# The weights of the first norm: one row and two matmuls in place of a load of 128 equal rows

## The chip, the cores and the metric

The kernel runs on 1 core of one Trainium2 chip. The metric is the device time of one execution in microseconds (us). The kernel before took 2623.56 us (median of 3 runs, 2621.81 to 2627.48 us).

## What is computed

One layer of an encoder trunk on a sequence of 2048 frames with 1024 features, all in float32: token mixing (one projection of the normed input, whose columns go to sliding-window attention with sinks and to a gated linear recurrence, then one output projection), cross-attention into 256 memory tokens, and a SwiGLU feed-forward part. Each of the three stands between two RMS norms with their own weights. The change touches the first norm of all:

```python
def rms_norm(x, g):
    xf = x.astype(jnp.float32)
    y = xf * lax.rsqrt(jnp.mean(xf * xf, axis=-1, keepdims=True) + RMS_EPS)
    return (y * g.astype(jnp.float32)).astype(x.dtype)

    u = rms_norm(h, g_mix_pre[l])
    z = u @ w_in[l]
    ...
```

`g_mix_pre` is one row of 1024 float32 numbers, drawn around 1.

## The kernel before

The work is written against a tile framework: the program lists instructions with the tiles that they read and write, and a planner, which simulates the engines' times, orders the instructions of each engine, picks the buffers and sets all semaphores. So the order on an engine may differ from the order of the text. Each engine then runs its own list strictly in order. All loads and stores of this stage are issued by one queue, that of SyncE (SP), and also in order.

Every large product is done in three float32r matmuls: each operand is split into a high part (a copy rounded to float32r) and a low part (what is left), and high x high, high x low and low x high are added in PSUM (`products`, L1017 to L1019). Most products go block by block through a seven-product scheme, the first two blocks of the input projection through a plain one (`eight`).

`in_first` (L413) does the first half of the input projection, 1024 frames in two groups `s` of four tiles of 128 frames. A frame lies in a partition, so a tile is 128 x 1024 and the norm's weights have to stand in all 128 partitions. The steps of the first 40 us are:

- `x_loads` (L418) loads tiles of x, 512 KB each, into `stage[s]`, a tile of 128 x 4 x 1024 with the tag "T" (three buffers, which the split operands of later blocks use after it). Right behind the first tile of x, it calls `gain` (L88), which loads the weights into the tile `g_mix` from a source with a zero step over the partitions: 128 equal rows of 4 KB, 512 KB in all. All these loads pass through `load`, L75.
- `x0_j`, called `junk`, is the second tile of tag "T". Its only use is to take the squares that nobody reads.
- `normed` (L406) norms one tile in place: ScalarE squares it into `junk` and sums (L409), GpSimd makes the reciprocal root in two small operations (`rstd`, L102 and L104), and VectorE multiplies x by the root and by `g_mix` (L411). The 16 tiles of the first and the second half (L411 in both cases) all read `g_mix`.
- `flipped` (L431) transposes the normed tile on TensorE (L440) into two PSUM banks. `first` (L452) splits them into the high and low parts (L457 on ScalarE, L458 on VectorE); `copied` and `later` keep a float32 copy for later sums (L446) and split that (L888 on GpSimd, L889 on VectorE).
- The weights of the projection (`in_w_in`) come in blocks of 512 rows x 256 columns as `sraw` and are split into `S` by `streamed` and `split2` (L886 on ScalarE or L888 on GpSimd, then L889 on VectorE).

PSUM in this stage has six banks with the tag "m" and two with the tag "s"; `bank("s")` and `bank("h")` both take the latter two in turn.

Of the kernel before, what the change touches and what calls it, by code (L numbers as in the profile page):

```python
# [11 lines left out]
F32 = mybir.dt.float32  # L12
F32R = mybir.dt.float32r
I32 = mybir.dt.int32
AF = mybir.ActivationFunctionType
# [3 lines left out]
P = 128  # L19
T = 2048  # L20
D = 1024
# [15 lines left out]
def f32(ap):  # L37
    return ap.bitcast(F32)
# [10 lines left out]
class Layer:  # L49
# [363 lines left out]
    def in_first(self):  # L413

        nc, I = self.nc, self.I
        stage = []

        def x_loads(s, tiles):  # L418
            if tiles[0] == 0:
                stage.append(self.tb.tile([P, 4, D], F32, tag="T", name=f"x0_{s}", bufs=3))  # L420
            for i in tiles:
                self.load(stage[s][:, i, :], I["x"][(4 * s + i) * P:(4 * s + i + 1) * P, :])
                if s + i == 0:
                    self.g_mix = self.gain(I["g_mix_pre"])

        x_loads(0, (0, 1))
        junk = self.tb.tile([P, 4, D], F32, tag="T", name="x0_j", bufs=3)
        T, raw = {}, {}
        key = {(0, 0): 1, (1, 0): 2, (0, 1): 8, (1, 1): 3}

        def flipped(s, i, kinds):  # L431

            x = stage[s][:, i, :]
            self.normed(x, junk[:, i, :])
            banks = []
            for q in range(2):
                ps = self.bank(kinds[q])
                for j in range(4):
                    k = 4 * q + j
                    nc.tensor.transpose(ps[:, j * P:(j + 1) * P], x[:, k * P:(k + 1) * P], self.ident)  # L440
                banks.append(ps.rearrange("p (j t) -> p j t", j=4))
            return banks

        def copied(s, i, banks):
            for q in range(2):
                nc.scalar.activation(raw[q, s][:, :, i * P:(i + 1) * P], banks[q], AF.Copy)  # L446

        def parts(s, i, q):
            o = slice(i * P, (i + 1) * P)
            return T[key[q, s]][:, 0, :, o], T[key[q, s]][:, 1, :, o]  # L450

        def first(i, kinds):  # L452

            banks = flipped(0, i, kinds)
            for q in range(2):
                hi, lo = parts(0, i, q)
                nc.scalar.activation(hi, banks[q], AF.Copy)  # L457
                nc.vector.tensor_tensor(lo, banks[q], f32(hi), ALU.subtract)  # L458
            return banks

        def later(i):
            banks = flipped(1, i, "sh")
            copied(1, i, banks)
            for q in range(2):
                self.split2(raw[q, 1][:, :, i * P:(i + 1) * P], *parts(1, i, q), "P")

        for s in range(2):
            for q in range(2):
                self._n += 1
                raw[q, s] = self.pair_tile().rearrange("p a d -> p (a d)").rearrange("p (k t) -> p k t", k=4)  # L470
        for q in range(2):
            for s in range(2):
                T[key[q, s]] = self.big.tile([P, 2, 4, 512], F32R, tag="big", name=f"u0_{q}{s}")
        second = {}

        def fetch():
            for s in range(2):
                for q in range(2):
                    r = self.pair_tile().rearrange("p a d -> p (a d)").rearrange("p (k t) -> p k t", k=4)
                    self.load(r, self.un_d[4 * q:4 * q + 4, :, s * 512:(s + 1) * 512].rearrange("k p t -> p k t"))  # L480
                    second[q, s] = r
                    yield

        beside = [(), (0,), (1, 2), (3,), (4,), (5,), (6,), (7,), (), (), ()]
        get = fetch()
        blocks = [("q" if i == 0 else "p" if i < 2 else "s",)
                  + self.in_block(*p, beside[i], get if i > 9 else (), None if i else lambda: x_loads(0, (2, 3)))
                  for i, p in enumerate(self.ORDER)]
        phases = self.phases([(lambda i, j, a, n: raw[i, j][:, a:a + n, :], 4, blocks, None, {})], T)
        next(phases)  # L490
        x_loads(1, range(4))
        b0 = first(0, "sh")
        b1 = first(1, "gt")
        next(phases)
        b2 = first(2, "gt")
        copied(0, 0, b0)
        b3 = first(3, "sh")
        copied(0, 1, b1)
        copied(0, 2, b2)
        copied(0, 3, b3)  # L500
        next(phases)
        for i in range(4):
            later(i)
        self.mix_consts()
        for _ in phases:
            pass
        for _ in get:
            pass
        u = []
        for s in range(2):  # L510
            u.append([])
            for q in range(2):
                self._n += 1
                t = self.big.tile([P, 2, 4, 512], F32R, tag="big", name=f"u1_{q}{s}")
                r = second[q, s]
                for k in (0, 2):
                    self.split2(r[:, k:k + 2], t[:, 0, k:k + 2], t[:, 1, k:k + 2], "A")
                u[s] += [(t[:, 0, k, :], t[:, 1, k, :]) for k in range(4)]
        return u
# [1090 lines left out]
```

## Time and profile before

| | us | share of the span |
|---|---|---|
| median of 3 runs | 2623.56 | |
| the profiled execution | 2629.38 | |
| its span | 2627.7 | |
| TensorE matmuls busy | 2560.7 | 97% |
| VectorE busy | 1732.1 | 66% |
| ScalarE busy | 1262.0 | 48% |
| GpSimd busy | 431.3 | 16% |

In the rows of the profile, PE is TensorE, PEld its loads of stationary operands, DVE VectorE, ACT ScalarE, POOL GpSimd, and SPq the queue of SyncE that issues loads and stores. A row of the timeline has the start in us from the start of the span, the duration in us (from the first to the last of the instructions that were merged into it), the engine, the line, the operation, what it writes and reads, and how many instructions it stands for; in brackets is the time for which the engine had been idle before it, and what ended that. A row of DMA issues has the destination and source, the issuing queue, the count, the size, and the median time in us from issue to landing. A row of the windows has the stretch, its length, the busy time of each engine in it with the count of instructions, the granted clock of TensorE (1.00 is full), the busy share of the DMA engines and the rate.

The first 40 us read so: four loads are issued at once; x tile 0 lands and is squared; the weights land; VectorE norms; TensorE transposes; and the products of the first block begin at 16.82 us.

### The profile page before, as it was taken

The numbers are of one execution on the slowest core, as the hardware profiler recorded it, in microseconds if no ns is written. First come the engines' busy times: TensorE is split into PE (matmuls) and PEld (weight loads), VectorE is DVE, ScalarE is ACT, GpSimd is POOL, SyncE is SP. The second block draws the span as 40 slices with busy tenths as digits, with TensorE's granted clock in tenths as the row PEclk, the third lists the DMA queues.
The fourth block names the chain that finished last, engine by engine and source line by source line (L and its number), as shares of the span: only waits on it lengthen the run. The fifth ranks groups of instructions, "written<-read, shape, count | busy, mean of one in ns | idle before, by whom it ended". The sixth has DMA issues, their size and how long they took to land.

```text
span 2627.7 us, 34806 instructions
## 1 busy us (share of the span) xinstructions
PE 2560.7 (97%) x12329; PEld 2142.2 (82%) x12329; DVE 1732.1 (66%) x2725; ACT 1262.0 (48%) x2628; POOL 431.3 (16%) x627
## 2 busy tenths in 40 slices
PE   7999999999999999999989999999999999999998
PEld 6877888878988887888878888888888888888886
DVE  7675478877545778777676655566666556564656
ACT  5463366655545566565563333344333334453543
POOL 4231344331311332213310000000000000000022
PEclk9999999999999999999999999999999999999999
DMA  5445655675877886666884632353566434576888
GB/s 184 127 149 174 187 158 159 197 232 158 239 256 261 306 279 235 216 233 176 242 276 131 196 101 82 102 191 123 168 203 197 155 121 172 183 215 177 268 209 216
DMA packets 354158, 502.87 MB, mean 191 GB/s; under 512 B 20672, under 2 KB 237760, under 8 KB 353984
## 3 DMA queue, kind: packets, MB, share of 16 engines
q1 hardware_dynamic: 345632, 470.24, 55.0%
q0 software_dynamic: 8352, 30.41, 6.6%
q8 instruction: 97, 1.59, 0.3%
q14 instruction: 77, 0.63, 0.1%
HBM read 338.05 MB, written 162.53 MB: 191 GB/s over the span
## 4 chain that ended last, share of the span: by engine, by line
PE 81%; DMA 8%; DVE 4%; ACT 3%; issue 2%; POOL 1%; SPq 1%; DVEq 0%; POOLq 0%; ACTq 0%
PE psm L1017 23%; PE psm L1018 23%; PE psm L1019 23%; PE psg L158 2%; PE psg L157 2%; PE psg L156 2%; PE pss L1252 1%; DMA qd<-z_d 1%; DMA z<-in_w_out_dram 1%; DMA u_d<-row 1%; DMA qq<-z_d 1%; SPq L75 1%; DVE wlo L889 0%; DMA h_d<-row 0%; DMA row<-y_d 0%
## 5 line engine op out<-in xcount | busy, mean ns | idle before, releaser
L1017 PE MATMUL psm<-T,S 128*128 128x512 f32 x2699 | 1046.6, 392 | 18.7 <-ACT part L1032 9.4
L1018 PE MATMUL psm<-T,S 128*128 128x512 f32 x2699 | 1052.6, 391 | 0.7 <-DVE T L889 0.6
L1019 PE MATMUL psm<-T,S 128*128 128x512 f32 x2699 | 1042.7, 391 | 2.0 <-DVE S L889 2.0
L1017 PEld LDWEIGHTS psm<-T,S 128*128 128x128 f32 x2699 | 508.2, 188 | 129.7 <-ACT part L1032 10.6
L1019 PEld LDWEIGHTS psm<-T,S 128*128 128x128 f32 x2699 | 508.2, 188 | 108.3 <-DVE S L889 2.9
L1018 PEld LDWEIGHTS psm<-T,S 128*128 128x128 f32 x2699 | 508.3, 188 | 106.1 <-DVE T L889 2.1
L889 DVE TENSOR_TENSOR S<-sraw,S 128x512 fp32r<-128x512 f32 (+1 forms) x320 | 218.4, 689 | 215.9 <-ACT S L886 198.6
L886 ACT ACTIVATE S<-sum 128x512 fp32r<-128x512 f32 (+1 forms) x310 | 186.5, 620 | 345.0 <-PE psm L1019 257.9
L889 DVE TENSOR_TENSOR S<-sum,S 128x512 fp32r<-128x512 f32 (+1 forms) x368 | 246.8, 681 | 58.0 <-ACT S L886 34.6
L1032 ACT ACTIVATE part<-psm 128x512 f32<-128x512 f32 x270 | 159.9, 596 | 244.8 <-PE psm L1019 229.3
L886 ACT ACTIVATE S<-sraw 128x512 fp32r<-128x512 f32 (+1 forms) x273 | 168.0, 616 | 120.9 <-PE psm L1019 104.7
L1365 POOL DMA_DIRECT2D row<-y_d x28 | 25.8, 921 | 1124.4 <-DVE row L1541 1032.7
L889 DVE TENSOR_TENSOR T<-row,T 128x1024 fp32r<-128x1024 f32 (+1 forms) x122 | 143.7, 1191 | 66.5 <-ACT T L886 66.0
L156 PE MATMUL psg<-u,whi 128*128 128x512 f32 x352 | 141.5, 402 | 1.6 <-POOL whi L888 1.6
L158 PE MATMUL psg<-u,wlo 128*128 128x512 f32 x352 | 140.2, 398 | 0.9 <-DVE wlo L889 0.9
L157 PE MATMUL psg<-u,whi 128*128 128x512 f32 x352 | 140.3, 398 | 0.0
L886 ACT ACTIVATE T<-row 128x1024 fp32r<-128x1024 f32 x122 | 122.1, 1027 | 23.9 <-DVE row L915 7.8
L1336 ACT ACTIVATE junk<-row 128x512 f32<-128x512 f32 x160 | 99.9, 625 | 67.6 <-DVE row L1358 26.8
L888 POOL TENSOR_SCALAR S<-sum 128x512 fp32r<-128x512 f32 x58 | 48.3, 832 | 288.4 <-PE psm L1019 228.9
L1492 DVE TENSOR_TENSOR row<-psm,part 128x512 f32<-128x512 f32 x63 | 41.7, 688 | 59.5 <-PE psm L1019 59.4
L1501 DVE TENSOR_TENSOR part<-psm,part 128x512 f32<-128x512 f32 x60 | 39.8, 688 | 61.1 <-PE psm L1019 60.9
L156 PEld LDWEIGHTS psg<-u,whi 128*128 128x128 f32 x352 | 66.7, 189 | 14.7 <-POOL whi L888 2.1
(335 smaller groups left out, 3634.0 us busy)
## 6 DMA issues: line engine op xcount, KB each, us to landing
sraw<-in_w_gate_dram SPq DMA_DIRECT2D x44, 512.0 KB, 3.9
sraw<-in_w_up_dram SPq DMA_DIRECT2D x44, 512.0 KB, 4.0
hid_d<-row SPq DMA_DIRECT2D x44, 512.0 KB, 2.6
h_d<-row SPq DMA_DIRECT2D x32, 512.0 KB, 5.8
y_d<-row SPq DMA_DIRECT2D x32, 512.0 KB, 3.2
sraw<-hid_d SPq DMA_DIRECT2D x32, 512.0 KB, 5.1
row<-h_d POOLq DMA_DIRECT2D x30, 512.0 KB, 6.8
row<-u_d SPq DMA_DIRECT2D x30, 512.0 KB, 6.1
```

Source lines behind the costliest of these rows:

```text
L156: nc.tensor.matmul(ps, ah, bh, start=(i == 0), stop=False)
L157: nc.tensor.matmul(ps, ah, bl, start=False, stop=False)
L158: nc.tensor.matmul(ps, al, bh, start=False, stop=(i == n - 1))
L886: self.nc.scalar.activation(hi, raw, AF.Copy)
L888: self.nc.gpsimd.tensor_scalar(hi, raw, 1.0, 1.0, ALU.mult, ALU.mult)
L889: self.nc.vector.tensor_tensor(lo, raw, f32(hi), ALU.subtract)
L1017: nc.tensor.matmul(ps, s[:, 0, k, :], t[:, 0, k, :], start=st, stop=False, **kw)
L1018: nc.tensor.matmul(ps, s[:, 0, k, :], t[:, 1, k, :], start=False, stop=False, **kw)
L1019: nc.tensor.matmul(ps, s[:, 1, k, :], t[:, 0, k, :], start=False, stop=sp, **kw)
L1032: nc.scalar.activation(t, ps, AF.Copy)
L1336: self.nc.scalar.activation(junk, a, AF.Square, scale=float(D) ** -0.5, accum_out=to)
L1492: nc.vector.tensor_tensor(d, a, c, ALU.add)
```

## The change

The weights are loaded as one row of 4 KB into partition 0 of `junk`, ahead of the tiles of x. A row of 128 ones is written beside it. For each half of 512 columns, TensorE multiplies the ones (as a stationary operand of 1 x 128) with the half row (1 x 512) into a bank of the tag "s", which gives 128 equal rows, and ScalarE copies the bank to `g_mix`. Both operands are float32, so the weights pass unsplit. `junk` is asked for before `stage[0]`, so the two exchange places in the order of the "T" tiles.

```diff
             for i in tiles:
                 self.load(stage[s][:, i, :], I["x"][(4 * s + i) * P:(4 * s + i + 1) * P, :])
-                if s + i == 0:
-                    self.g_mix = self.gain(I["g_mix_pre"])
-
+
+        junk = self.tb.tile([P, 4, D], F32, tag="T", name="x0_j", bufs=3)
+
+        row, ones = junk[0:1, 2, :], junk[0:1, 3, 0:P]
+        self.load(row, I["g_mix_pre"][0:1, :])
         x_loads(0, (0, 1))
-        junk = self.tb.tile([P, 4, D], F32, tag="T", name="x0_j", bufs=3)
+        nc.vector.memset(ones, 1.0)
+        self.g_mix = self.gain_tile()
+        for q in range(2):
+            ps = self.bank("sh"[q])
+            sl = slice(q * 512, (q + 1) * 512)
+            nc.tensor.matmul(ps, ones, row[:, sl], start=True, stop=True)
+            nc.scalar.activation(self.g_mix[:, sl], ps, AF.Copy)
         T, raw = {}, {}
```

## The prediction

> **What bounds the kernel now.** I read the page's busy times first, then the busy time by stretches of the span.
>
> ```profile
> span 2627.7 us, 34806 instructions
> PE 2560.7 (97%) x12329; PEld 2142.2 (82%) x12329; DVE 1732.1 (66%) x2725; ACT 1262.0 (48%) x2628; POOL 431.3 (16%) x627
> ```
> ```profile
> core 0: us, PE busy (x) PEld busy (x) DVE busy (x) ACT busy (x) POOL busy (x), PEclk, DMA share, GB/s
> 11.00:27.90 16.90, 13.37 (x78) 12.48 (x79) 16.76 (x23) 13.95 (x28) 11.06 (x16) 1.00 0.96 285
> ...
> 40.00:110.00 70.00, 70.00 (x317) 58.08 (x318) 50.24 (x59) 30.27 (x49) 13.70 (x20) 1.00 0.49 156
> 110.00:700.00 590.00, 569.58 (x3050) 483.75 (x3049) 435.28 (x896) 321.04 (x808) 181.75 (x257) 0.99 0.60 178
> 700.00:1000.00 300.00, 288.77 (x1611) 249.39 (x1610) 188.81 (x232) 165.66 (x364) 70.40 (x102) 0.99 0.82 273
> ```
>
> The kernel as a whole is bound by matmuls: TensorE is busy for 97% of the span, and for 70.00 of 70 us between 40 and 110 us. But the change lies in the first 10 us, and there the limit is another one: from 11 to 27.9 us VectorE is busy for 16.76 of 16.90 us. So the question is when VectorE's unbroken run of work begins, and whether the matmuls behind it move with it. The timeline answers the first part. It is shown by engine: ScalarE, GpSimd, VectorE, TensorE.
>
> ```profile
> 4.08 1.06 ACT L409 ACTIVATE x_j<-x 128x1024 f32<-128x1024 f32 x1 [2.00 <-DMA x<-in_x_dram]
> 5.04 0.19 ACT L409 ACTIVATION_READ_ACCUMULATOR x_j<-x 128x1 f32 x1
> 7.85 1.06 ACT L409 ACTIVATE x_j<-x 128x1024 f32<-128x1024 f32 x1 [2.63 <-DMA x<-in_x_dram]
> ...
> 5.59 0.56 POOL L104 TENSOR_TENSOR n_r<-n_v,mhalf 128x1 f32<-128x1 f32 x1
> 8.91 0.62 POOL L888 TENSOR_SCALAR S<-sraw 128x512 fp32r<-128x512 f32 x1 [2.76 <-DMA sraw<-in_w_in_dram]
> 10.39 0.56 POOL L104 TENSOR_TENSOR n_r<-n_v,mhalf 128x1 f32<-128x1 f32 x1
> ...
> 6.62 1.28 DVE L411 SCALAR_TENSOR_TENSOR x<-x,n_r,g 128x1024 f32<-128x1024 f32 x1 [5.00 <-DMA g<-in_g_mix_pre_dram]
> 9.56 0.69 DVE L889 TENSOR_TENSOR S<-sraw,S 128x512 fp32r<-128x512 f32 x1 [1.66 <-POOL S L888]
> 10.98 1.28 DVE L411 SCALAR_TENSOR_TENSOR x<-x,n_r,g 128x1024 f32<-128x1024 f32 x1 [0.73 <-POOL n_r L104]
> 26.59 1.28 DVE L458 TENSOR_TENSOR u<-pss,u 128x512 fp32r<-128x512 f32 x2
> ...
> 27.33 0.39 PE L1018 MATMUL psm<-u,S 128*128 128x256 f32 x1 [1.22 <-DVE u L458]
> 39.87 0.98 PE L1017 MATMUL psm<-u,S 128*128 128x512 f32 x3 [0.93 <-POOL u L888]
> ```
>
> The load of the weights ends a wait of 5.00 us on VectorE at 6.62, and that is what the change takes away. It isn't the gate, though: GpSimd had the root of tile 0 ready at 5.59 + 0.56 = 6.15, so only 0.47 us of the wait is the weights' own, and VectorE then idles again. Its unbroken run begins with the norm of tile 1 at 10.98. Behind that stand the root of tile 1 (10.39) and, in GpSimd's order, the split of the first weight block (8.91), which waited for its DMA; the squares of tile 1 (7.85) waited for a DMA too. At the far end of the run, the split at 26.59 releases TensorE at 27.33, and TensorE's last wait of this stretch ends at 39.87. With no idle time in the 70 us after that, a shift of VectorE's run should arrive at the end one for one.
>
> **What is removed: 512 KB in the queue.** The issues on SP's queue, and then their times to landing (x tile 0, the weights, x tile 1, the first weight block):
>
> ```profile
> 0.80 0.39 SPq L75 DMA_DIRECT2D x<-in_x_dram  x1
> 1.24 0.42 SPq L75 DMA_DIRECT2D g<-in_g_mix_pre_dram  x1
> 1.71 0.42 SPq L75 DMA_DIRECT2D x<-in_x_dram  x1
> 2.18 1.12 SPq L75 DMA_DIRECT2D sraw<-in_w_in_dram  x2
> ```
> ```profile
> x<-in_x_dram SPq DMA_DIRECT2D x1, 512.0 KB, 3.3
> ...
> g<-in_g_mix_pre_dram SPq DMA_DIRECT2D x1, 512.0 KB, 5.3
> ...
> x<-in_x_dram SPq DMA_DIRECT2D x1, 512.0 KB, 6.1
> ...
> sraw<-in_w_in_dram SPq DMA_DIRECT2D x1, 256.0 KB, 6.7
> ...
> lb<-in_hgrn_lb_dram SPq DMA_DIRECT2D x1, 4.0 KB, 8.9
> ...
> on_raw<-in_hgrn_onorm_dram SPq DMA_DIRECT2D x1, 0.5 KB, 5.1
> ```
>
> Issue plus landing gives 0.80 + 3.3 = 4.10 for x tile 0, 1.24 + 5.3 = 6.54 for the weights, 1.71 + 6.1 = 7.81 for x tile 1 and 2.18 + 6.7 = 8.88 for the weight block: the 512 KB of weights took 6.54 - 4.10 = 2.44 us of the queue, the equal 512 KB of x behind them 7.81 - 6.54 = 1.27 us. Without them, all that comes later lands between 1.27 us (if they cost as x does) and 2.44 us earlier: x tile 1 at 5.4 to 6.5, the weight block at 6.4 to 7.6. One issue takes the place of another, so x tile 1 is issued when it was. Only x tile 0 goes behind the row, by one issue (1.24 - 0.80 = 0.44 us), and lands at 4.1 to 4.54.
>
> **What is added: row, matmuls, copies.** No row of the trace shows a 4 KB load on an empty queue. The bounds are the shortest load or store of all that touch a tile named g, 2.1 us, and x tile 0 with its 512 KB, 3.3 us; the small loads above, 5.1 and 8.9 us, stood in a full queue and serve for a rival. I take 2.5 us, nearer to the shortest since the row has the queue to itself, and the row lands at 0.80 + 2.5 = 3.3 (2.9 to 4.1).
>
> ```profile
> DMA to landing us min/median/max: 2.1/4.7/10.3
> ```
> ```profile
> 7.96 1.97 PE L440 MATMUL pss<-ident,x 128*128 128x128 f32 x8 [7.96 <-DVE x L411]
> 22.09 1.03 PE L440 MATMUL pss<-ident,x 128*128 128x128 f32 x8
> ...
> 361.65 1.46 PE L785 MATMUL psh<-qq,k 128*128 128x192 f32 x8
> ...
> 19.38 0.60 ACT L446 ACTIVATE pair<-psm 128x512 f32<-128x512 f32 x1
> ...
> 1.00 0.48 DVE L368 MEMSET reset<- 128x512 f32 x1
> ```
>
> The ones cost VectorE less than the 0.48 us of a memset of four times the width, in its idle time before 6.62. For a plain float32 matmul of 512 columns, the nearest row is L785: eight records in 1.46 us, two to a matmul, so 0.365 us for 192 columns and 0.97 us for 512. That was with TensorE warm. The same eight transposes took 1.97 us at 7.96 and 1.03 us at 22.09, so an array that has just begun works 1.91 times slower, and the two matmuls cost 1.86 us each. A lower bound is 0.39 us, the matmul of 256 columns at 27.33. With 1.8 us each: the first ends at 5.1, the second at 6.9. A copy of 128x512 out of PSUM takes 0.60 us, so `g_mix` is complete at 7.5; with all lower bounds at 2.9 + 2 x 0.39 + 0.6 = 4.3, with all upper ones at 4.1 + 2 x 1.86 + 0.6 = 8.4. Before, it was 6.54.
>
> [...]
>
> **The sum.** ScalarE runs its list in order, so it matters where the planner puts the two copies. That it moves work is seen in the memset at 1.00, whose text stands behind all of this stage. If the squares of tile 0 aren't held by both copies, they run at about 4.5 to 5.7 or behind the first copy to 6.9, and tile 0 is normed when `g_mix` is there, at some 7.6 to 8.9. Squares with the sum behind them take 5.04 + 0.19 - 4.08 = 1.15 us. Those of tile 1 need x at 5.4 to 6.5 and follow the second copy, from 7.5 to 8.65. From their end (7.85 + 1.15 = 9.0) to the norm it takes 10.98 - 9.0 = 1.98 us now, because the split of the weight block is in GpSimd's way; without it the root is there 6.15 - 5.23 = 0.92 us after the squares, and that block now lands by 7.6 and is split before. So tile 1 is normed at about 9.5 in place of 10.98: **1.5 us earlier**. This lies inside the 1.27 to 2.44 us by which the DMAs behind move up, so the later tiles follow. ScalarE's 1.2 us of copies and TensorE's 3.7 us lie in time in which both wait for x (4.08, 7.96); without that cover each would cost its own length. The exchange of the "T" buffers costs nothing:
>
> ```profile
> 21.86 1.09 ACT L409 ACTIVATE x_j<-x 128x1024 f32<-128x1024 f32 x1
> ...
> 42.00 3.50 DVE L915 TENSOR_TENSOR pair<-pair,pair 128x1024 f32<-128x1024 f32 x3
> ```
>
> `junk` is last written at 21.86, and the work for the first new "T" tile begins at 42.00; if it had to wait, the next late thing would be the split at L886. The term is then 0 - 1.5 = -1.5 us, with bounds 0 and -2.44. The profiled execution, 2629.38 us (1.7 us more than its span), would become 2627.9. It is 5.8 us above the median and above all three runs, so I put the same shift on the median: 2623.56 - 1.5 = **2622.1 us**, 2621 to 2623.6 by the bounds.
>
> **The rivals.** *The copies stand ahead of all squares* (they do in the text). Then tile 0 is squared at 7.5 to 8.65, its root is there at 9.6, it is normed from 9.6 to 10.9, and tile 1 follows at 10.9: as before, 2623.5 us. The transfer is saved and the time is spent on ScalarE. For it speaks the text's order; against it, that x tile 0 lands at 4.5, when ScalarE has nothing else to do.
>
> *The row lands late.* The same order on ScalarE, but the row takes as long as the small loads in the trace: with 5.1 us `g_mix` is complete at 10.1 and all moves by 2.6 us, with 8.9 us at 13.9 and by 6.4 us: 2626.2 to 2630.0 us, slower. It decides from the moment when `g_mix` is later than 7.5 and ScalarE is held by it. Against it: both small loads were issued into a queue that was moving 285 GB/s, and the row comes first.
>
> *The planner orders later work differently.* The change shifts its simulated times at the very start, and its choices depend on them. Nothing can be gained from 40 to 110 us, but TensorE idles for 590 - 569.58 = 20.4 us and 300 - 288.77 = 11.2 us in the two stretches from 110 to 1000 us, where attention and recurrence run beside the projections. A different order there that removes a quarter of these 31.6 us gives about 2615.6, one that adds a quarter 2631.5. For it speaks that the order is made by simulation; against it, that TensorE's 70 full microseconds let the other engines fall back to the same state relative to it.
>
> **How the numbers follow.** A measurement of this kernel can tell about 0.2%, 5.2 us, from no change: its three runs spread over 5.7 us. Forecast 0.38 and the copies ahead 0.18 both end within it. The late row has 0.07, 0.03 of it beyond 5.2 us. The other order has 0.37: 0.16 faster, 0.15 slower, 0.06 within. So faster 0.16, same 0.38 + 0.18 + 0.04 + 0.06 = 0.66, slower 0.15 + 0.03 = 0.18. The range must hold 0.8, so it takes in both ends of the other order at a quarter of the idle time and a little beyond, 2613 to 2633 us; the forecast's own range is 2621 to 2623.6.
>
> **What the changed profile would show.** The row lands near 3.3 us; two matmuls of about 1.8 us and two copies of 0.6 us before 7.6 us; x tile 1 lands at 5.4 to 6.5; VectorE's unbroken run begins near 9.5 and the release of TensorE that was at 27.33 comes near 25.8; from 40 us on all rows have the same order, some 1.5 us earlier. The prediction is wrong if tile 1 is normed after 10.98, if the 1.5 us are there at 40 us and gone at 110 us, or if TensorE's idle time from 110 to 1000 us differs from 31.6 us by more than 5 us.

## The result and the profile after

The changed kernel took 2634.32 us in the median of 18 runs (2626.75 to 2640.36), the kernel before 2628.40 us beside it (18 runs, 2621.81 to 2632.98). The ratio is 1.0023, with a 95% interval of 1.0014 to 1.0031: **6.0 us slower** (3.7 to 8.1, the interval times 2628.4). The profiled execution took 2635.37 us. Its head of the page, and its windows (columns as before):

```profile
span 2633.7 us, 34818 instructions
PE 2561.5 (97%) x12333; PEld 2140.2 (81%) x12333; DVE 1732.8 (66%) x2726; ACT 1262.7 (48%) x2630; POOL 435.2 (17%) x627
```
```profile
11.00:27.90 16.90, 14.94 (x92) 14.16 (x91) 15.79 (x23) 13.59 (x28) 9.45 (x16) 1.00 0.86 257
40.00:110.00 70.00, 69.31 (x307) 57.46 (x308) 49.08 (x58) 29.72 (x48) 14.12 (x19) 0.96 0.44 143
110.00:700.00 590.00, 567.82 (x3048) 481.83 (x3048) 436.98 (x897) 323.08 (x811) 185.78 (x258) 0.99 0.60 178
700.00:1000.00 300.00, 286.70 (x1625) 247.84 (x1623) 188.48 (x233) 164.94 (x362) 71.01 (x102) 1.00 0.82 273
```

The busy times are those of before; no engine has more to do. What stands out is the second window: TensorE is granted 0.96 of its clock from 40 to 110 us, where it had 1.00. The stage that the change edits, in the timeline of the changed kernel (lines of the code behind the edit are 8 higher than before): TensorE, ScalarE, GpSimd, VectorE.

```profile
2.32 3.75 PE L434 MATMUL pss<-x_j 1*128 1x512 f32 x4 [2.32 <-DMA x_j<-in_g_mix_pre_dram]
...
5.18 1.06 ACT L409 ACTIVATE x_j<-x 128x1024 f32<-128x1024 f32 x1 [3.11 <-DMA x<-in_x_dram]
6.24 0.58 ACT L435 ACTIVATE g<-pss 128x512 f32<-128x512 f32 x1
6.71 1.04 ACT L409 ACTIVATE x_j<-x 128x1024 f32<-128x1024 f32 x1
7.75 0.58 ACT L435 ACTIVATE g<-pss 128x512 f32<-128x512 f32 x1
...
7.41 0.62 POOL L896 TENSOR_SCALAR S<-sraw 128x512 fp32r<-128x512 f32 x1 [0.16 <-DMA sraw<-in_w_in_dram]
8.89 1.48 POOL L104 TENSOR_TENSOR n_r<-n_v,mhalf 128x1 f32<-128x1 f32 x1
...
8.67 1.28 DVE L411 SCALAR_TENSOR_TENSOR x<-x,n_r,g 128x1024 f32<-128x1024 f32 x1
10.40 1.28 DVE L411 SCALAR_TENSOR_TENSOR x<-x,n_r,g 128x1024 f32<-128x1024 f32 x1 [0.45 <-POOL n_r L104]
26.54 0.69 DVE L466 TENSOR_TENSOR u<-pss,u 128x512 fp32r<-128x512 f32 x1
```

The row does its part: the weights are complete at 7.75 + 0.58 = 8.33, and tile 1 is normed at 10.40 in place of 10.98. But at 26.54 VectorE begins the last of these splits, which it began at 26.59 before: little is left of the gain, and the lists of the two kernels no longer agree. Two losses lie behind it. The first is at 30 to 48 us. TensorE and the granted clock, before and then after:

```profile
37.78 1.15 PE L1252 MATMUL pss<-ident,pair 128*128 128x128 f32 x8 [0.19 <-ACT pair L446]
```
```profile
34.00:41.00 7.00, 5.42 (x37) 4.06 (x36) 6.07 (x6) 4.36 (x8) 6.08 (x7) 1.00 0.07 19
41.00:44.00 3.00, 3.00 (x15) 2.46 (x14) 2.97 (x4) 0.68 (x1) 0.00 (x0) 1.00 0.47 133
```
```profile
35.03 1.15 PE L448 MATMUL pss<-ident,x 128*128 128x128 f32 x8 [0.20 <-ACT pair L454]
37.04 0.66 PE L448 MATMUL pss<-ident,x 128*128 128x128 f32 x4 [0.86 <-ACT pair L454]
40.69 1.65 PE L1025 MATMUL psm<-u,S 128*128 128x512 f32 x3 [2.99 <-POOL u L896]
46.37 1.04 PE L1260 MATMUL pss<-ident,pair 128*128 128x128 f32 x8
```
```profile
34.00:41.00 7.00, 2.95 (x21) 2.09 (x19) 6.19 (x6) 3.82 (x8) 6.69 (x9) 0.86 0.00 1
41.00:44.00 3.00, 3.00 (x8) 2.32 (x8) 2.96 (x5) 0.00 (x0) 0.65 (x1) 0.50 0.00 0
44.00:48.00 4.00, 4.00 (x20) 3.32 (x19) 4.00 (x5) 2.05 (x4) 0.00 (x0) 0.77 0.00 0
```

The planner made another order for the end of the first stage. Before, ScalarE squares the first tile of the second half at 31.99, and TensorE transposes it at 37.78, in the gap in which it waits for the splits of the next operand. Now the squares come at 35.36, GpSimd's root of that tile, at 37.62, stands ahead of its last splits, and the transposes stand at 46.37, behind the products. TensorE waits 2.99 us in place of 0.93. Its granted clock is half from 38.98 to 45.81, 6.8 us, and for the last 45.81 - 40.69 = 5.12 of them it works. So 40.69 - 39.87 = 0.82 us of later start, about 0.9 us of transposes no longer in a gap, and half of 5.12 = 2.56 us make 4.3, an estimate from these rows. The next landmark, the transposes x8 of the next tile, moves by 4.06, from 100.79 to 104.85:

```profile
100.79 1.04 PE L1252 MATMUL pss<-ident,pair 128*128 128x128 f32 x8
```
```profile
104.85 1.03 PE L1260 MATMUL pss<-ident,pair 128*128 128x128 f32 x8
```

The instructions of all engines behind that stand in one order in both kernels, except for two of ScalarE near 270 us. And yet a second loss comes there, at 250 to 300 us. SP, TensorE, GpSimd and VectorE, before and after:

```profile
255.81 2.31 SPq L75 DMA_DIRECT2D raw<-in_w_in_dram  x3
...
261.29 0.50 PE L156 MATMUL psg<-u,whi 128*128 128x512 f32 x1 [1.65 <-POOL whi L888]
262.96 0.50 PE L158 MATMUL psg<-u,wlo 128*128 128x512 f32 x1 [0.94 <-DVE wlo L889]
...
259.92 1.32 POOL L888 TENSOR_SCALAR whi<-raw 128x1024 fp32r<-128x1024 f32 x1 [14.60 <-DMA raw<-in_w_in_dram]
...
257.37 2.36 DVE L889 TENSOR_TENSOR u<-pair,u 128x1024 fp32r<-128x1024 f32 x2 [0.26 <-ACT u L886]
259.64 2.13 DVE L561 SCALAR_TENSOR_TENSOR pair<-th,pair 128x512 f32<-128x512 f32 x2
261.70 1.21 DVE L889 TENSOR_TENSOR wlo<-raw,whi 128x1024 fp32r<-128x1024 f32 x1
```
```profile
248.20 6.49 SPq L75 DMA_DIRECT2D raw<-in_w_in_dram  x3
...
267.15 0.79 PE L158 MATMUL psg<-u,wlo 128*128 128x512 f32 x1 [5.01 <-DVE wlo L897]
...
259.69 1.89 POOL L896 TENSOR_SCALAR whi<-raw 128x1024 fp32r<-128x1024 f32 x1
261.53 2.02 POOL L821 TENSOR_TENSOR W<-W,G 128x512 f32<-128x512 f32 x1
...
259.43 3.21 DVE L897 TENSOR_TENSOR u<-pair,u 128x1024 fp32r<-128x1024 f32 x2 [0.26 <-ACT u L894]
262.57 2.55 DVE L569 SCALAR_TENSOR_TENSOR pair<-th,pair 128x512 f32<-128x512 f32 x2
265.04 2.06 DVE L897 TENSOR_TENSOR wlo<-raw,whi 128x1024 fp32r<-128x1024 f32 x1
```

Although the kernel is late, the three `raw` loads of the next stage are issued 7.6 us **earlier**. So GpSimd's work on them falls beside VectorE's splits of the present stage, and the same three VectorE rows take 3.21 + 2.55 + 2.06 = 7.82 us in place of 2.36 + 2.13 + 1.21 = 5.70. TensorE waits for the last of them, 5.01 us in place of 1.65 + 0.94: 2.4 us lost.

### The profile page after: what moved, and what is told of

Read it like the earlier page. It is cut to its first block, busy times and chain, and to the rows that moved or that the text cites. A ratio compares the mean times of both kernels' runs of the same rounds, so it can differ in the third digit from the quotient of the medians.

```text
span 2633.7 us, 34818 instructions
## 1 busy us (share of the span) xinstructions
PE 2561.5 (97%) x12333; PEld 2140.2 (81%) x12333; DVE 1732.8 (66%) x2726; ACT 1262.7 (48%) x2630; POOL 435.2 (17%) x627
## 3 DMA queue, kind: packets, MB, share of 16 engines
q8 instruction: 97, 1.59, 0.3%
## 4 chain that ended last, share of the span: by engine, by line
PE 82%; DMA 8%; DVE 4%; ACT 3%; issue 2%; POOL 1%; SPq 1%; DVEq 0%; POOLq 0%; ACTq 0%
PE psm L1025 23%; PE psm L1027 23%; PE psm L1026 23%; PE psg L158 2%; PE psg L157 2%; PE psg L156 2%; PE pss L1260 1%; DMA row<-y_d 1%; DMA qd<-z_d 1%; DMA u_d<-row 1%; DMA z<-in_w_out_dram 1%; DVE wlo L897 0%; DMA z_d<-z 0%; SPq L75 0%; DMA out_s<-u 0%
## 5 line engine op out<-in xcount | busy, mean ns | idle before, releaser
L158 PEld LDWEIGHTS psg<-u,wlo 128*128 128x128 f32 x352 | 67.0, 190 | 18.5 <-DVE wlo L897 5.4
```

The costliest lines, as they stand in the source:

```text
L158: nc.tensor.matmul(ps, al, bh, start=False, stop=(i == n - 1))
```

## The experiments

Three suspects, then: the order of the first stage, whatever lets the `raw` loads go early, and the pair of ScalarE. To follow them, two landmarks are compared with before: the transposes x8 at 100.79, and the copy `z<-psg` of ScalarE at 297.47. Their shifts in us, from one profile each, with the ratio of the times (five rounds each, beside the kernel before on the same chip):

| kernel | order of stage 1 | x8 (100.79) | z (297.47) | ratio (95%) |
|---|---|---|---|---|
| the change | new | +4.06 | +4.41 | 1.0023 (1.0014 to 1.0031) |
| after_again | new | +3.65 | +3.82 | 1.0015 (1.0006 to 1.0025) |
| row_slots | new | +3.76 | +6.08 | 1.0020 (1.0010 to 1.0029) |
| row_gain | new | +4.14 | +4.28 | 1.0024 (1.0012 to 1.0036) |
| load_new_order | new | +3.93 | +4.04 | 1.0012 (1.0003 to 1.0021) |
| row_filled | new | +1.35 | +0.73 | 1.0021 (1.0012 to 1.0031) |
| row_third | its own | +1.19 | +1.80 | 1.0007 (0.9998 to 1.0016) |
| row_old_order | before's | -1.25 | +0.32 | 1.0009 (1.0001 to 1.0018) |
| row_slots_old_order | before's | +0.39 | +2.00 | 1.0004 (0.9995 to 1.0014) |
| row_gain_old_order | before's | +0.29 | +2.25 | 1.0007 (0.9995 to 1.0019) |
| load_slots | before's | +0.28 | +2.91 | 1.0013 (1.0001 to 1.0025) |
| swap | before's | +0.24 | -2.19 | 0.9996 (0.9987 to 1.0005) |
| row_all_back | before's | -1.17 | -1.78 | 0.9987 (0.9978 to 0.9996) |

Three things limit what the table can tell. The intervals of the ratios reach 2 to 3 us to either side, as far as most terms. A single profile has stretches of 3.4 or 6.8 us of half clock near 144 and 265 us that come and go with the same instructions (the kernel before has them at 144.09 and 263.56, the change at 264.26 alone; `swap`, in effect the kernel before, has a clock of 1.00 from 255 to 295 us and gains 2.2 us by 297). And the profiled executions aren't typical ones: those of `after_again`, `row_filled` and `row_old_order` are the shortest of their runs, that of `load_new_order` is the longest. Behind 297 us they wander further: `after_again`, 3.8 us late there, has a span of 2624.1 us, and the kernel before 2627.7. So what arrives at the end is told by the ratios alone, and each term below is read at its own place, from the wait that carries it.

**Row or order.** Two kernels cross them. The first is the change with before's order of the first stage, the second the kernel before with the changed one's; the order is laid down as dependencies without semaphores between neighbours on an engine:

```diff
+    def in_order(self, *chains):
+        traced = {i.name: i for i in self.nc.cur_bb.bb.instructions}
+        info = mybir.DependencyInfo(mybir.DependencyClass.NoSync, mybir.DependencyReason.DATA)
+        for c in chains:
+            for x, y in zip(c, c[1:]):
+                self.tc.add_manual_dep(traced[f"I-{y}"], f"I-{x}", info, reason="in_order")
...
+        self.in_order([...], [...], [...], [...])
         u = []
```

> The change as it is, with the order of the kernel before laid down for VectorE, ScalarE, GpSimd and TensorE over the first stage (its own matmuls and copies stay where they were). If the planner's other order costs the time, the transposes of the second-half tile of x at L1252 that began at 100.79 us in the kernel before and at 104.85 in the changed one begin at about 100.2 (tile 1 was normed 0.58 us earlier), there is no half-rate stretch of TensorE's clock near 40 us, and the time is that of before or up to 1 us less: ratio 0.9996 to 1.0000. If the row, the matmuls and the copies cost it themselves, or the later x tile 0, the transposes begin at 103 or later and the ratio stays at 1.0015 to 1.0023.

> The kernel before with its 512 KB load, with the changed kernel's order laid down for the four engines over the first stage. If the order costs the time, TensorE waits 2 to 4 us for the splits on GpSimd near 40 us, its clock falls to half for a window or two, the transposes of L1252 begin at 102.5 to 106 us in place of 100.79, and the ratio is 1.0010 to 1.0025. If the row, the matmuls and the copies cost it, nothing changes: 100.8 us, ratio 1.0000.

TensorE in `row_old_order`, then in `load_new_order`:

```profile
38.65 0.96 PE L1051 MATMUL psm<-u,S 128*128 128x512 f32 x3 [0.92 <-POOL u L922]
```
```profile
40.74 1.65 PE L1043 MATMUL psm<-u,S 128*128 128x512 f32 x3 [3.00 <-POOL u L914]
```

The order alone, without the row, costs +3.93 at the first landmark, with the wait and the half clock: TensorE waits 3.00 us before the products at 40.74, and is granted 0.50 from 41 to 44 us. The row alone gains 1.25 there, and its TensorE waits 0.92 us as before. That settles the first loss, and the ratio of `load_new_order` (1.0012) lies in its range. That of `row_old_order` (1.0009) doesn't: the second loss wasn't expected in either text. `row_old_order` lost 2.4 us between 250 and 297 us, `load_new_order` nothing.

The pair also shows where the row's gain went. In the new order, with the row and without it, TensorE works without a gap from the transposes at 18.10 (19.69 without the row) to those at 33.7. The row is 1.59 us ahead at their start; 5 us on, the two kernels are level, with the row first:

```profile
18.10 1.09 PE L448 MATMUL pss<-ident,x 128*128 128x128 f32 x4 [1.29 <-DVE x L411]
23.63 0.60 PE L448 MATMUL pss<-ident,x 128*128 128x128 f32 x4
```
```profile
23.66 0.60 PE L447 MATMUL pss<-ident,x 128*128 128x128 f32 x4
```

The four transposes at 18.10 take 1.09 us, those at 23.63 only 0.60. In the changed kernel, the products of 256 columns begin 0.21 us apart until its first clock record, at 21.92, and 0.12 us apart behind it: up to there it works at about half rate. (Ahead of its first record, the clock column of a window shows 1.00: it does so from 14 to 21 us here.) `load_new_order` takes 23.66 - 19.69 = 3.97 us for this stretch, where the changed kernel takes 23.63 - 18.10 = 5.53. Since `load_new_order` is one execution, whether it is the row that delays the clock isn't shown. So with the new order the row gains nothing by 100 us: +3.65 to +4.14 with it, +3.93 without.

**The place of the row, and the half clock.** `row_third` issues the row behind both tiles of x; `row_filled` has the change's order laid down, and ten more matmuls in the wait of 2.99 us, whose results the next product overwrites:

```diff
-        self.load(row, I["g_mix_pre"][0:1, :])
         x_loads(0, (0, 1))
+        self.load(row, I["g_mix_pre"][0:1, :])
```
```diff
         x, y = self.bank("g"), self.bank("t")
+        for _ in range(10 if halves else 0):
+            self.nc.tensor.matmul(x, a11[:, 0, 0, :], T[1][:, 0, 0, :], start=True, stop=True, skip_group_check=True)
         self.products(x, [(a11, T[8], nk)], True, False)
```

> The change with the row loaded behind both tiles of x, so x tile 0 is issued at 0.80 us again; left to itself the planner then orders the end of the first stage as in the kernel before and only its beginning otherwise. If the order at the end of the stage costs the time, the transposes of L1252 begin at 100 to 101 us and the ratio is 0.9996 to 1.0004. If the matmuls and the copies cost it, they begin at 104 or later and the ratio is 1.0015 or more; if the late x tile 0 did, this run recovers its 1.1 us alone: 103.7.

> The changed kernel with its own order laid down, and ten further matmuls of 128x512 whose result is overwritten, on TensorE in the wait of 2.99 us ahead of 40.69 us. If half of the loss is the clock that falls after this wait, there is no half-rate stretch near 40 us and the transposes of L1252 begin at about 102.3 us (104.85 less half of the 5.1 us from 40.69 to 45.81 at half rate). If the clock costs nothing, they begin at 104.9 or later, since the ten matmuls take 2.3 us of the wait.

TensorE in `row_filled`:

```profile
37.09 2.54 PE L1124 MATMUL psm<-u,S 128*128 128x512 f32 x10
40.33 0.96 PE L1051 MATMUL psm<-u,S 128*128 128x512 f32 x3 [0.70 <-POOL u L922]
```

With the array kept at work, the clock is 1.00 through that stretch (34 to 48 us), and the first landmark is at 102.14, 2.71 us ahead of the change; 0.36 of this is there when the products begin (40.33 against 40.69), which leaves 2.35 where the arithmetic had 2.56. So the half clock follows from the wait, and is worth about that. In the ratio this gain isn't found: it is 1.0021, where 2.7 us less would be 1.0013. The interval just holds that, and the point stays open.

With the row in third place, the planner changes the order only as far as the 67th place of TensorE's list, some 24 us, and there is no half clock near 40 us either (1.00 from 40 to 110 us). Its text is missed by a little (101.98 and 1.0007): behind two tiles of x the row lands at 5.63 only, and tile 0 is normed at 10.87. Of the 14 profiles of this study, the five with the new order and nothing in the gap have it there, the other nine don't.

**What lets the raw loads go.** The first idea was the order in which `junk` and `x0_0` are allocated. `swap` is the kernel before with only that exchanged, `row_slots` the change with it put back, `row_slots_old_order` the same with before's order:

```diff
+        junk = self.tb.tile([P, 4, D], F32, tag="T", name="x0_j", bufs=3)
         x_loads(0, (0, 1))
-        junk = self.tb.tile([P, 4, D], F32, tag="T", name="x0_j", bufs=3)
```

> The kernel before, with its load of 128 rows and its instructions in their order on every engine, but with the scratch tile junk allocated ahead of x0_0, as the change has it: the two change places in memory and nothing else. Theory (the exchange of the two tiles costs time, though far behind the first stage): at the transposes of L1252 x8 (100.79 before) nothing is changed, within 0.4; the three loads of raw near 255.8 are issued some 6 to 10 us earlier, TensorE's wait near 262 is some 5 us for VectorE's wlo in place of 1.65 + 0.94, and by the third z<-psg of ScalarE near 297 (297.47 before) the kernel is 2.0 to 2.9 us late. Ratio some 1.0009. Rival (the loss behind 250 us comes from the two ScalarE instructions that stand the other way round near 270 us, or from the row): the raw loads stay near 255.8, nothing is lost between 250 and 300 us, ratio 1.0000.

> The change with x0_0 allocated ahead of junk, so that both lie where the kernel before has them; the order of instructions is the changed kernel's own. Theory (order of the first stage +4, exchange of the tiles +2.4, row -1.25, and no others): 104.85 at the transposes x8 as with the change, the wait near 262 us as before (1.65 + 0.94), no further loss between 250 and 300 us, ratio some 1.0012 to 1.0016 against the change's 1.0023. Rival (the exchange costs nothing): 2 us more are lost between 250 and 300 us, and the ratio is the change's, 1.0021 or more.

> The change with x0_0 allocated ahead of junk and with the order of the kernel before laid down for the first stage (PE, VectorE, ScalarE, GpSimd), so that the row and its matmuls are all that is left of it beside the two ScalarE instructions near 270 us. Theory: the transposes x8 at 99.4 to 99.7 (100.79 before), still 1.0 to 1.5 us ahead at 297 us, ratio 0.9994 to 0.9998. Rival (the loss between 250 and 300 us belongs to the ScalarE exchange or to the row): 99.5 at the transposes, then 2 us lost by 297 us, ratio 1.0003 to 1.0009 as with the tiles exchanged.

> The changed kernel once more, beside the others. If the order of the first stage is what costs it: the wait of some 3 us before TensorE's products of L1025 near 40.7 us is there again and the granted clock is near 0.5 behind it for some 6.8 us, the transposes x8 at 104.85 within 0.5, and the wait of 5 us near 267. If the half rate was an accident of one execution: no such clock near 40 us, the transposes at some 102.3. Ratio 1.0014 to 1.0031 either way.

The first three missed. The order of allocation does nothing to the memory: a tile gets its place when it is first used, and in the program the three edits moved no address. So `swap` is the kernel before once more (0.9996), `row_slots` the change, and `row_slots_old_order` is `row_old_order`; they serve as repeats. `after_again` met its text: the wait, the half clock (0.50 from 41 to 44 us) and 104.44 are there again.

What does set the addresses is the load of the row: its target lies in `junk`, which so becomes the first "T" tile in use and gets the place that `x0_0` had. In the built program, a `raw` tile of the next stage lies in that place, and its load waits for the last matmul that reads the "T" tile there: it waits for TensorE's semaphore to reach 1110 before, and 1066 after. Three kernels test it. `load_slots` is the kernel before with a dead load of the row into `junk` in front and the order unchanged; `row_gain` and `row_gain_old_order` are the change with the row landing in `g_mix` itself, so that `junk` isn't the first:

```diff
+        junk = self.tb.tile([P, 4, D], F32, tag="T", name="x0_j", bufs=3)
+        self.load(junk[0:1, 2, :], I["g_mix_pre"][0:1, :])
         x_loads(0, (0, 1))
```
```diff
-        row, ones = junk[0:1, 2, :], junk[0:1, 3, 0:P]
+        ones = junk[0:1, 3, 0:P]
+        self.g_mix = self.gain_tile()
+        row = self.g_mix[0:1, :]
```

> The kernel before with its load of 128 rows and its order laid down for the first stage, and with one dead load of 4 KB added ahead of all others: the row, into the scratch tile junk, read by nothing. With it junk is the first of the T tiles to be used and takes the memory that x0_0 has before, as in the changed kernel; allocating junk first (swap, row_slots) had left the memory as it was, since a tile takes its place when it is first used. Theory (the loss of 2.0 to 2.9 us between 250 and 300 us comes from that memory: the raw tiles of the next stage lie in it, and are loaded when the T tile there is read for the last time): at the transposes x8 of L1252 within 1 of before's 100.79; the raw loads near 246 to 248 in place of 255.8, one wait of some 5 us for VectorE's wlo near 262, GpSimd's whi beside VectorE's splits, and 2.0 to 2.9 us lost by the third z<-psg near 297. Ratio 1.0007 to 1.0013. Rival (the two ScalarE instructions exchanged near 270 us, which this kernel has as before): nothing lost there, ratio 1.0000 to 1.0003.

> The change with its row landing in partition 0 of the tile of the norm weights itself, so that the T tile that the raw tiles follow is as before, and with before's order laid down for the first stage. Theory: at the transposes x8 99.5 (a half-rate stretch of TensorE's clock in the first 40 us would make it up to 101.2), raw loads near 254 and the waits of 1.65 and 0.94 as before, nothing lost between 250 and 300 us, so that a gain of 0 to 1.3 us stays: ratio 0.9994 to 1.0001, at or below before and below the 1.0004 to 1.0009 of the same order with the row in junk. Rival (ScalarE's exchange near 270 us, which this kernel still has, is the cause): raw loads near 254, yet 2.0 to 2.9 us lost by 297 us, ratio 1.0004 to 1.0010.

> The same placing of the row, with the order that the planner makes, which is the changed kernel's. Theory (order +4, memory +2.4, row about -1): 104.4 to 104.9 at the transposes x8 (the half clock near 41 us with it), raw loads some 4 us behind before's 255.8, nothing more lost by 297 us; ratio 1.0011 to 1.0016, some 0.0008 under the change's. Rival (memory costs nothing): 2.0 to 2.9 us more lost by 297 us, ratio 1.0020 or more.

SP and TensorE in `load_slots`, then SP, TensorE and ScalarE in `row_gain_old_order`:

```profile
246.86 6.06 SPq L75 DMA_DIRECT2D raw<-in_w_in_dram  x3
...
265.91 0.61 PE L158 MATMUL psg<-u,wlo 128*128 128x512 f32 x1 [4.82 <-DVE wlo L915]
```
```profile
255.53 2.28 SPq L75 DMA_DIRECT2D raw<-in_w_in_dram  x3
...
261.00 0.50 PE L156 MATMUL psg<-u,whi 128*128 128x512 f32 x1 [1.66 <-POOL whi L923]
262.68 0.79 PE L158 MATMUL psg<-u,wlo 128*128 128x512 f32 x1 [0.94 <-DVE wlo L924]
282.70 0.50 PE L156 MATMUL psg<-u,whi 128*128 128x512 f32 x1 [1.03 <-ACT z L640]
...
281.53 0.63 ACT L704 ACTIVATE qs<-qd 128x512 fp32r<-128x512 f32 x1 [4.29 <-DMA qd<-z_d]
282.07 1.07 ACT L640 ACTIVATE z<-psg 128x512 f32<-128x512 f32 x2
```

The exchange of the places alone brings the early loads and the wait of 4.82 us into a kernel that has nothing else of the change: the theory holds, and the ratio of 1.0013 lies at the upper end of what was expected. In the program, the places of six tiles are all that differs from before, with the dead load: x0_0, `junk`, x0_1 and the three "T" tiles behind them. (In `row_third`, x0_0 keeps its place, but the new "T" tiles stand as in the change, and the loads leave at 245.02: it is these tiles that decide, and not `junk`.) Put right, the loads are back at 255.53 and the waits are 1.66 and 0.94. But `row_gain_old_order` was still 2.25 late at 297, its ratio of 1.0007 lies in the rival's range, and the rival was right in part: the two ScalarE instructions cost time when the wait near 262 does not. A copy of PSUM, `z<-psg`, now stands behind `qs<-qd`, which waits for its DMA until 281.53; so TensorE, short of a bank, waits 1.03 us. In `row_gain` it is 0.66. In the change itself TensorE has no such wait: it seems that the 5.01 us near 267 had given that DMA the time it needed. The rest, some 1.2 us in both, comes at 262 to 270 us, where the half clock lasts 6.8 us in place of 3.4. In the ratio `row_gain` stayed where the change is (1.0024, against 1.0011 to 1.0016 expected): a miss of the expectation, with an interval that reaches down to 1.0012.

**All taken back.** `row_all_back` has the row in `g_mix`, before's order of the first stage, and ScalarE's pair as before:

```diff
+                self.in_order([2323, 2448])
                 for _ in hgrn:
                     pass
```

> row_gain_old_order with the last difference taken back too: the ScalarE copy z<-psg (L605 before) stands ahead of the second qs<-qd near 270 us again, as in the kernel before. Only the row in place of the 128 equal rows, with its two matmuls and two copies, is left of the change. Theory (that exchange cost row_gain_old_order the wait of 1.03 us for ScalarE's z near 282 us): no wait for z there, at the transposes x8 99.5 to 101.2, and at 297 us between -1.5 and +1.2 of before's 297.47, the spread being that of the landings in the first 10 us and of the half-rate stretch of TensorE's clock near 265 us; ratio 0.9993 to 1.0005, no longer apart from before. Rival (the row itself, its cold matmuls or something not seen costs time): no less late at 297 us than row_gain_old_order's +2.25, ratio 1.0007 or more.

TensorE twice, then ScalarE:

```profile
99.62 1.03 PE L1288 MATMUL pss<-ident,pair 128*128 128x128 f32 x8
261.22 0.54 PE L158 MATMUL psg<-u,wlo 128*128 128x512 f32 x1 [0.94 <-DVE wlo L925]
...
295.69 0.60 ACT L641 ACTIVATE z<-psg 128x512 f32<-128x512 f32 x1 [4.80 <-PE psg L158]
```

No wait for `z`, 1.17 us ahead at the first landmark and 1.78 at the second, and 2625.74 us against 2630.28 beside it: 0.9987 (0.9978 to 0.9996), below the range that was expected. The row by itself is faster than the load, by some 1 to 2 us in this trace. The ratio says 3.4 us, but the 2630.28 is the highest of the five medians of the kernel before (the lowest is 2626.03), and `row_gain_old_order`, with the same row and order at the start, had +0.29 at 100 us. So that the row gains is likely, and how much isn't settled.

## Why the prediction was wrong

It said -1.5 us, and it is +6.0; the 2634.3 us lie just above the range of 2613 to 2633. Part of that distance is luck: the three runs that the range was built on had a median of 2623.56, the 18 runs of the same kernel 2628.40, and 6.0 us on top of the former would have been within it. What failed is the sign, and the two steps below.

**What held.** The two cold matmuls: 3.75 us for both, 1.87 each against 1.86. The gate is VectorE's run, not the wait of 5.00 us. The shift isn't lost as far as 297 us: `row_all_back` has 1.17 us at 100 us and 1.78 there. Of the 0.6 between, 0.5 come at two waits of TensorE, 0.44 us in place of 0.64 near 118 us and 2.60 in place of 2.94 near 141. That it arrives at the end one for one, no profile can show. And -1.5 us for the row itself: -1.25 and -1.17 where the order is before's. Even that isn't certain in every execution. `row_gain_old_order` has +0.29, since its weight block landed later (8.48 against 7.27 in `row_all_back`) and GpSimd's split of it, 1.66 us in place of 0.62, held up the root of tile 1 (normed at 11.60), and `row_slots_old_order` +0.39, with a half-rate stretch of its own from 26 to 30 us (a clock of 0.72 from 26 to 32 us).

**Sizes that were off, without deciding anything.** The row landed at 2.32, ahead of its bounds of 2.9 to 4.1. x tile 0 was there at 5.18 and not at 4.1 to 4.54. Why isn't settled: it was 4.65 in `load_slots`, with the row ahead and the weights behind it, and 4.62 in `row_third`, with only x tile 1 at its heels. `g_mix` was complete at 8.33 and not 7.5, because the second copy was put behind the squares of tile 1.

**The first step that failed** is "the later tiles follow". The working let the planner move two copies and a memset in the first 10 us, and took the rest of the stage's order as given. The planner reordered TensorE's list from about the 29th to the 275th place, and the loss of 4 us lay at 30 to 46 us. The rival "the planner orders later work differently" named the right cause, with a chance of 0.37, of which 0.15 for slower, and in the wrong place: it priced the idle time from 110 to 1000 us, because only there the profile showed slack. But the slack that a new order can destroy also lay at 27 to 40 us, where before has waits of 1.22 and 0.93 us. And its counterargument held: behind 110 us, the order was the same but for two instructions. The loss was more than double what a lost gap costs (0.82 + 0.9 us), because the clock fell.

**The second step that failed** is "The exchange of the 'T' buffers costs nothing". The rows quoted for it asked whether the next "T" tile has to wait for `junk`, and it does not. What decides is the other end: when the tile in that place is read for the last time, and what is laid there afterwards. The exchange freed the memory of a `raw` tile earlier, and the price, 2.2 to 2.4 us, came from a load that went *too soon*. The -1.5 for the row itself falls out of the sum, since the new order leaves nothing of it. With +4.0 for the order and +2.4 for the memory, the change comes to +6.4 at 297 us. Three profiles show +4.4, +3.8 and +6.1; in the first, TensorE keeps its full clock near 144 us (1.00 from 143 to 148 us), where the kernel before has 3.4 us of half clock (0.66 there), worth up to 1.7. The ratio says +6.0 (3.7 to 8.1).

Of the signs named in advance, that the 1.5 us are there at 40 us and gone at 110 was the nearest; it came as 0.58 us at tile 1, and 0.82 us of delay at 40.69. The idle time from 110 to 1000 us is 22.18 + 13.30 = 35.5 us in place of 31.6. This is 3.9 us more and stays under the 5 us set as a limit, though 2.4 us of real loss are in it. Why the planner prefers the new order wasn't isolated, beyond that it does so with the row ahead of x and not with the row behind two tiles.

## What to carry to other kernels

Where a planner orders the work, an edit of the first microseconds has to be priced over the whole stretch in which the order differs, and the places to look at are the gaps that now hold useful work. When two buffers change places, look at who reads each of them last and what is laid there next: a load that can go earlier may put one engine's work beside another's. And a small gain is worth its price only with the old order and the old places held; here this turned +6 us into what is probably a small gain.

## What was not expected of the hardware

A wait of 2.99 us cost TensorE's clock for 6.8 us, the last 5.1 of which it spent at work: half rate from 38.98 to 45.81 us, twice the 3.41 us of the shortest such stretch. In `row_slots` the half clock in the same place lasted some 3.4 us (0.99 from 34 to 41 us, 0.50 to 44 and 0.96 to 48). In the 3.41 us ahead of 38.98, TensorE was not idle: it transposed until 36.18 and from 37.04 to 37.70, 1.27 us in all, a share of 0.37.

In the profiles of the kernel before and of the change, all stretches of full and of half clock, but for the last of each, last a multiple of 3.413 us. Cut into pieces of that length, in step with each profile's own clock records, the two hold 1507 pieces at full clock. The clock fell behind all 13 in which TensorE was busy (by the modelled ends of its matmuls) for less than 0.47, behind 1 of the 5 with 0.48 to 0.53, and behind none of the rest. From half, it came back behind all 12 pieces with more than 0.92, and behind none of the 8 with 0.77 or less. So a wait did not have to fill a piece, and its length alone did not settle it: ahead of 263.56, waits of 1.65 and 0.94 us left the kernel before a share of 0.39 in one piece, and the clock fell; a wait of 2.57 us that ended at 146.53 in the change lay across two, with shares of 0.76 and 0.49, and it stayed.

VectorE's splits took 3.21 us beside GpSimd's work in place of 2.36, and 2.06 in place of 1.21. Not every one was longer: of the two `u<-pair,u`, the one at 259.43, beside GpSimd's `whi<-raw` for 0.97 us, took 1.23 us as before, and only the one at 260.58 took 2.07 in place of 1.22. The rows that grew read `pair` and `u`, `th` and `pair`, `raw` and `whi`; `pair<-th,psm`, with one input in PSUM, took 0.68 us at 267.02 in the change, 0.55 of it beside GpSimd's `kk<-kk,G` (265.98 to 267.57), and 0.67 us at 262.83 before, 0.40 of it beside `whi<-raw`. What in this makes the difference isn't shown.
